# A two-layer encoder on one core: one block product's left operand split a half earlier, first operands fed ahead of the last relu, transposes spread out

## The chip, the core and the metric

The kernel runs on 1 core of one Trainium2 chip, in one launch. The metric is the device time in microseconds (us); lower is better. The engines are called PE (matmul), PEld (its weight load), DVE, ACT, POOL and SP; each works through its own list of instructions in order, and waits on semaphores for the others. A queue name such as SPq or ACTq in a row means that this engine issued a DMA.

## The reference: what is computed

Two rows of 512 tokens (prompt and sample) go through two encoder layers. Each layer has a token mixer, a LayerNorm, a squared-ReLU MLP, and a second LayerNorm:

```python
for l in range(DEPTH):                                # DEPTH = 2, D_MODEL = 1024, D_FF = 4096
    h = x @ w_in[l]
    aq, ak, av, hq, hf_f, hf_b, hi, hg, ga, gb = jnp.split(h, cuts, axis=-1)
    ...
    o_att = window_attention(q, k, v, att_sink[l])
    o_hg = hgrn2_branch(hq, hf_f, hf_b, hi, hg, lower[l], hgrn_norm_g[l])
    mixed = jax.nn.sigmoid(ga) * (o_att @ w_proj_att[l]) + jax.nn.sigmoid(gb) * (o_hg @ w_proj_hgrn[l])
    ...
```

What follows is `layer_norm(ALPHA * x + mixed @ w_out)`, then `layer_norm(ALPHA * x + relu(x @ w_ff1)**2 @ w_ff2)`. All in float32.

## The kernel before, in words

**Products.** A float32 operand is split into a rounded part ("hi", a cast on ACT) and the rest ("lo", a subtraction on DVE or POOL); a product is three matmuls, hi by hi, hi by lo, lo by hi. A projection of 512 tokens on 128 columns is 24 matmuls (`mm3`, L152 to L154). `load_w` loads 512 KB of weights (SP, L143) into one of 3 `raw` tiles and splits them (L131 hi, L132 lo) into one of 3 `w` tiles. `Fm.put(j, rows)` turns 128 finished rows of the activations into columns: 8 transposes on PE (L180), 2 casts on ACT (L185), 2 subtractions on DVE (L186).

**The MLP.** Its first half, `ff1`, makes the 4096 hidden columns in 16 pairs of 256. For each pair `combine` (L904 on) forms sums and differences of four 128x512 tiles, and `spill` writes them to DRAM (`hsp`), since the second product is done by a scheme with seven block products in place of eight. They are the phases M1, M2, M5, M3, M6, M4, M7 of the list `PHASES`, each with 16 steps k, one step for each pair; a step is 12 matmuls (`products`, L971 to L973). `operands` prepares a step's two factors: the left one is loaded from `hsp` into a `raw` tile (SP, L950, 256 KB), the right one is a sum of two blocks of `w_ff2` (POOL, L961); both are then split into a `w` tile, together 128x1024 (L131 on ACT, L132 on DVE). `feed(i)` calls `operands` two steps ahead. M7 is the last phase. Its left factor is the difference of the tiles h2 and h3.

**The end of a layer.** `fold` (L981) adds a finished block to the rows in `acc`. Rows 4 to 7 (of 128 tokens each) are complete when M4 ends, so their LayerNorms (`close`) are called in the steps k = 1, 4, 7, 10 of M7. The last 4 steps of M7 are kept back (`TAIL`, with operands in `X` tiles) and done row by row for rows 0 to 3, with `close` of each row behind the next row's products. A LayerNorm ends with an addition on POOL (L211). `close` then stores: in the first layer to `x_res` (SP, L998) and `put` of the row into the next layer's columns; in the last layer one half of the row by SP and one by ACT (L996). The next layer begins with `prep(0)`: projections on the columns FF, FB and HQ, each for the tokens 512 to 1023 and then for 0 to 511.

**Order.** A scheduler places the instructions on each engine; an engine's order is that of the rows printed in the section on the change, not that of the code.

Of the kernel before, what the change touches and what calls it, by code (L numbers as in the profile page):

```python
# [42 lines left out]
H_M1, H_M2, H_M5, H_M6, H_M7, H_M4, H_M3 = range(7)  # L43
# [44 lines left out]
def tile_encoder_trunk(  # L88
# [17 lines left out]
    hsp = [dram.tile([PAIRS, P, 7, 512], F32, name=f"hsp{l}") for l in range(DEPTH)]  # L106
# [123 lines left out]
    def hgrn(l, x, gate):  # L230
        with tc.tile_pool(name=f"hg{l}", bufs=1) as hp:
# [39 lines left out]

            def prep(p, u):
                for col in (C_FF, C_FB, C_HQ, C_HI, C_HG):
                    if l == 0 and p == 0 and col == C_FF:
                        w = w_first
                    else:
                        w = load_w(
                            [w_in[l][:, col + p * P:col + (p + 1) * P]],
                            *((nc.vector.tensor_copy, nc.vector) if l == 0 and p == 0 and col in (C_FB,) else ()),
                        )  # L280
                    for g in (range(NG), (1, 0))[l > 0 and p == 0]:
                        ps = project(w, x, g)
                        r = u[g]
                        if col in (C_FF, C_FB):
                            d = int(col == C_FB)
                            if not d:
                                r["f"] = hp.tile([P, 2, SEQ], F32, tag="F", name="F", bufs=2)
                                r["k"] = hp.tile([P, 2, SEQ], F32, tag="K", name="K", bufs=4)
                            f = r["f"][:, 1 - d]
                            nc.scalar.activation(out=f, in_=ps, func=AF.Sigmoid)  # L290
                            if l:
                                nc.gpsimd.tensor_scalar(
                                    f, f, oml[:, d, p:p + 1], lb[:, d, p:p + 1], op0=ALU.mult, op1=ALU.add
                                )
                            nc.gpsimd.tensor_scalar(r["k"][:, d], f, -1.0, 1.0, op0=ALU.mult, op1=ALU.add)
                        elif col == C_HQ:
                            sg = t2k()
                            nc.scalar.activation(out=sg, in_=ps, func=AF.Sigmoid)
                            q = t2k()
                            nc.vector.scalar_tensor_tensor(  # L300
                                q, ps, 0.125, sg, op0=ALU.mult, op1=ALU.mult
                            )
                            r["q"] = hp.tile([P, 2, SEQ], F32, tag="Q", name="Q", bufs=4)
                            nc.vector.tensor_tensor(
                                r["q"], q.unsqueeze(1).to_broadcast([P, 2, SEQ]), r["f"], op=ALU.mult
                            )
                            ox = r["ox"] = hp.tile([P, SEQ], F32, tag="ox", name="ox", bufs=4)
                            nc.vector.tensor_tensor(ox, r["k"][:, 0], r["k"][:, 1], op=ALU.add)
                            nc.vector.tensor_tensor(ox, ox, q, op=ALU.mult)
                        elif col == C_HI:  # L310
                            vt = t2k()
                            nc.scalar.copy(vt, ps)
                            ps = sm_ps()
                            for c in range(4):
                                s = slice(c * P, (c + 1) * P)
                                nc.tensor.transpose(ps[:, s], vt[:, s], ident)
                            v = hp.tile([P, 4, P], F32, tag="V", name="V", bufs=2)
                            nc.scalar.copy(v, ps)
                            r["v"] = v
                            pairs(r, vt)  # L320
                        else:
                            sg = t2k()
                            nc.scalar.activation(out=sg, in_=ps, func=AF.Sigmoid)
                            hg = hp.tile([P, SEQ], F32, tag="hg", name="hg", bufs=2)
                            nc.vector.tensor_tensor(hg, ps, sg, op=ALU.mult)
                            r["hg"] = hg
                        yield
# [447 lines left out]

    for l in range(DEPTH):
# [20 lines left out]
        with tc.tile_pool(name=f"ff{l}", bufs=1) as fp:  # L797
# [98 lines left out]
            def ff1(f, out):  # L896
# [186 lines left out]
```

## Time and profile before

| what | us |
|---|---|
| median of 3 runs | 3065.37 (3060.91 to 3068.12) |
| the profiled execution | 3064.09 |
| its span in the trace | 3062.3 |
| PE busy | 2956.7 (97% of the span) |
| DVE, ACT, POOL busy | 1666.7, 1090.9, 865.8 |

The span is that of the trace's instructions; 1.8 us of the profiled execution lie outside it. A busy share is a mean over stages that are bound by different engines. All numbers ahead of the result come from this one execution, whose granted TensorE clock was 0.988 of full speed in the mean.

### The profile page before, as it was taken

The page shows a single profiled execution, that of the slowest core. Times are in us where ns is not written, and L with a number is a line of the kernel's source. Part 1 is how long each engine was busy: PE and PEld are TensorE (multiplying, and loading weights), DVE is VectorE, ACT ScalarE, POOL GpSimd, SP SyncE. Part 2 cuts the span into 40 slices and gives each one's busy share as a digit, 9 for nine tenths or more (in the row PEclk, how much of TensorE's full clock was granted, in tenths as well). Part 3 has the DMA queues.
Part 4 walks back from the last instruction along what each step waited for, and adds up shares of the span by engine and source line. Part 5 has one row for each costly group of instructions (what it writes and reads, how often), then busy time and mean ns, then how long its engine had stood idle before and what let it go on. Part 6 is the DMA issues. An engine that isn't in the chain of part 4 may idle for free.

```text
span 3062.3 us, 42748 instructions
## 1 busy us (share of the span) xinstructions
PE 2956.7 (97%) x16720; PEld 2399.4 (78%) x16720; DVE 1666.7 (54%) x2877; ACT 1090.9 (36%) x1826; POOL 865.8 (28%) x532
## 2 busy tenths in 40 slices
PE   8999999999999999999889999999999999999997
PEld 6777787877888887888667777878878888878885
DVE  5888748126543333445768887481265433344448
ACT  3344447323121112433434444473231211124333
POOL 4222120112222222454542221101231222234544
PEclk9999999999999999999999999999999999999999
DMA  3111232246123346533321112322460243564333
GB/s 127 36 42 36 67 89 69 80 162 218 34 86 134 132 167 241 169 97 97 113 75 36 42 36 69 90 64 100 157 226 9 93 144 125 177 255 144 97 97 107
DMA packets 278890, 331.98 MB, mean 108 GB/s; under 512 B 16545, under 2 KB 185121, under 8 KB 274593
## 3 DMA queue, kind: packets, MB, share of 16 engines
q1 hardware_dynamic: 276816, 325.00, 32.5%
q10 hardware_dynamic: 1872, 4.26, 0.4%
q8 instruction: 131, 2.15, 0.3%
q14 instruction: 71, 0.57, 0.1%
HBM read 230.38 MB, written 92.27 MB: 105 GB/s over the span
## 4 chain that ended last, share of the span: by engine, by line
PE 81%; DVE 10%; DMA 3%; issue 3%; POOL 1%; ACT 1%; SPq 0%; ACTq 0%; POOLq 0%; DVEq 0%
PE mm L152 17%; PE mm L154 16%; PE mm L153 16%; PE sm L971 3%; PE sm L972 3%; PE sm L973 3%; PE mm L972 3%; PE mm L971 3%; PE mm L973 3%; PE mm L864 2%; PE mm L866 2%; PE mm L865 2%; PE sm L695 1%; PE sm L641 1%; PE sm L685 1%
## 5 line engine op out<-in xcount | busy, mean ns | idle before, releaser
L152 PE MATMUL mm<-X,w 128*128 128x512 f32 x2624 | 1033.4, 394 | 4.8 <-ACT w L131 4.1
L153 PE MATMUL mm<-X,w 128*128 128x512 f32 x2624 | 1028.7, 392 | 0.0
L154 PE MATMUL mm<-X,w 128*128 128x512 f32 x2624 | 1026.2, 391 | 1.1 <-POOL w L132 1.1
L132 POOL TENSOR_TENSOR w<-raw,w 128x1024 fp32r<-128x1024 f32 (+1 forms) x179 | 417.9, 2336 | 1370.9 <-ACT w L131 1255.2
L152 PEld LDWEIGHTS mm<-X,w 128*128 128x128 f32 x2624 | 493.6, 188 | 111.8 <-ACT w L131 4.5
L154 PEld LDWEIGHTS mm<-X,w 128*128 128x128 f32 x2624 | 493.8, 188 | 102.3 <-POOL w L132 2.2
L153 PEld LDWEIGHTS mm<-X,w 128*128 128x128 f32 x2624 | 493.8, 188 | 98.6 <-DVE X L793 0.5
L131 ACT CAST w<-raw 128x1024 fp32r<-128x1024 f32 (+1 forms) x330 | 332.1, 1007 | 365.4 <-PE sm L973 106.7
L902 DVE TENSOR_TENSOR X<-t 128x512 f32<-128x512 f32 x128 | 88.6, 692 | 427.8 <-ACT t L901 427.8
L961 POOL TENSOR_TENSOR raw<-X 128x512 f32<-128x512 f32 x160 | 221.8, 1388 | 263.6 <-DVE w L132 259.4
L132 DVE TENSOR_TENSOR w<-raw,w 128x1024 fp32r<-128x1024 f32 x153 | 195.7, 1283 | 168.9 <-ACT w L131 168.7
L901 ACT ACTIVATE t<-mm 128x512 f32<-128x512 f32 x128 | 76.5, 598 | 554.7 <-PE mm L154 546.8
L971 PE MATMUL mm<-w 128*128 128x512 f32 x480 | 190.2, 397 | 11.3 <-ACT w L131 11.3
L972 PE MATMUL mm<-w 128*128 128x512 f32 x480 | 190.3, 396 | 3.7 <-DVE w L132 3.6
L973 PE MATMUL mm<-w 128*128 128x512 f32 x480 | 189.1, 394 | 0.0
L971 PE MATMUL sm<-w 128*128 128x512 f32 x384 | 149.5, 389 | 0.0
L973 PE MATMUL sm<-w 128*128 128x512 f32 x384 | 149.4, 389 | 0.0
L972 PE MATMUL sm<-w 128*128 128x512 f32 x384 | 149.4, 389 | 0.0
L793 DVE TENSOR_TENSOR X<-raw,X 128x512 fp32r<-128x512 f32 x32 | 20.8, 690 | 197.5 <-ACT X L792 197.4
L971 PEld LDWEIGHTS mm<-w 128*128 128x128 f32 x480 | 91.7, 191 | 32.0 <-ACT w L131 12.6
L864 PE MATMUL mm<-X 128*128 128x512 f32 x256 | 103.9, 406 | 11.2 <-DVE t L823 11.2
L959 POOL TENSOR_TENSOR w<-X,w 128x512 fp32r<-128x512 f32 x64 | 85.4, 1334 | 98.8 <-ACT w L955 98.6
(187 smaller groups left out, 3848.9 us busy)
## 6 DMA issues: line engine op xcount, KB each, us to landing
raw<-hsp SPq DMA_DIRECT2D x224, 256.0 KB
raw<-in_w_in_dram SPq DMA_DIRECT2D x84, 512.0 KB
raw<-in_w_ff_dram SPq DMA_DIRECT2D x64, 512.0 KB
hsp<-X SPq DMA_DIRECT2D x32, 1024.0 KB
X<-in_w_ff_dram SPq DMA_DIRECT2D x32, 1024.0 KB
gates<-gt SPq DMA_DIRECT2D x64, 256.0 KB
t<-gates SPq DMA_DIRECT2D x64, 256.0 KB
hsp<-X SPq DMA_DIRECT2D x32, 512.0 KB
```

Of the source, the lines that this page charges most:

```text
L131: (first or nc.scalar.copy)(hi, src)
L132: (eng or nc.gpsimd).tensor_tensor(lo, src, hi.bitcast(F32), op=ALU.subtract)
L152: nc.tensor.matmul(ps, ah, bh, start=(i == 0), stop=False)
L153: nc.tensor.matmul(ps, ah, bl, start=False, stop=False)
L154: nc.tensor.matmul(ps, al, bh, start=False, stop=(i == n - 1))
L864: nc.tensor.matmul(pend[j, n], mh, wh, start=(k == 0), stop=False)
L902: nc.vector.tensor_tensor(out[g], t, t, op=ALU.mult)
L959: nc.gpsimd.tensor_tensor(w[:, 1, 512:], src, w[:, 0, 512:].bitcast(F32), op=ALU.subtract)
L961: nc.gpsimd.tensor_tensor(raw[:, 512:], block(b0, k), block(b1, k), op=op)
L971: nc.tensor.matmul(ps[r], hh, wh, start=first, stop=False, **kw)
L972: nc.tensor.matmul(ps[r], hh, wl, start=False, stop=False, **kw)
L973: nc.tensor.matmul(ps[r], hl, wh, start=False, stop=stop, **kw)
```

## The change

Four things are changed.

1. M7's left factor is split in the first half: `combine` makes its hi (ACT) and lo (DVE) in the tiles where h1 and h2 stood, and `spill` writes 8 slots in two DMAs of 1 MiB, where it wrote 7 slots in three (1 MiB, 512 KB, 256 KB). In M7, `operands` loads both halves (512 KB) straight into the `w` tile, and splits only the right factor, 128x512.
2. `feed(0)` and `feed(1)` are called inside the last `ff1`, ahead of its projections, no longer behind the loop.
3. `put` of rows 4, 5, 6 is called a `close` later, that of row 7 after the first row of the tail, and those of rows 0 to 3 inside the next layer's first `prep`, whose columns now come as FF, FB, HQ for the tokens 512 to 1023 and then FF, FB, HQ for 0 to 511.
4. In the last layer both halves of rows 4 to 7 are stored by SP; rows 0 to 3 as before.

```diff
-H_M1, H_M2, H_M5, H_M6, H_M7, H_M4, H_M3 = range(7)
+H_M1, H_M2, H_M5, H_M6, H_M3, H_M7, H_M7L, H_M4 = range(8)
...
+            def columns(p):
+                cols = (C_FF, C_FB, C_HQ, C_HI, C_HG)
+                order = [(col, g) for col in cols for g in range(NG)]
+                if l and p == 0:
+                    order = [(col, 1) for col in cols[:3]] + [(col, 0) for col in cols[:3]] + order[6:]
+                ws = {}
+                for i, (col, g) in enumerate(order):
+                    if l and p == 0 and i == 3:
+                        for put in puts[2:]:
+                            put()
...
+                    yield col, g, ws[col]
+                    if l and p == 0 and i < 2:
+                        puts[i]()
...
             def ff1(f, out, before=()):
                 w = load_w([w_ff1[l][:, f * P:(f + 1) * P]])
+                for b in before:
+                    b()
...
                 nc.vector.tensor_tensor(h[:, 2], h[:, 2], h[:, 3], op=sub)
+                hi, lo = h[:, 1].bitcast(F32R), h[:, 2].bitcast(F32R)
+                nc.scalar.copy(hi, h[:, 2])
+                nc.vector.tensor_tensor(lo, h[:, 2], h[:, 1], op=sub)
 
             def spill(p, h, s):
                 nc.sync.dma_start(hid[p][:, H_M1:H_M6 + 1], s)
-                nc.sync.dma_start(hid[p][:, H_M7:H_M4 + 1], h[:, 2:4])
-                nc.sync.dma_start(hid[p][:, H_M3], h[:, 0])
+                nc.sync.dma_start(hid[p][:, H_M3:], h)
...
+                w = tile()
+                if slot == H_M7:
+                    nc.sync.dma_start(w[:, :, :512].bitcast(F32), hid[k][:, H_M7:H_M7L + 1])
+                    nc.gpsimd.tensor_tensor(raw[:, 512:], block(b0, k), block(b1, k), op=op)
+                    split(w[:, 0, 512:], w[:, 1, 512:], raw[:, 512:], nc.vector)
+                    return w
...
-                        (nc.sync, nc.scalar)[n].dma_start(yout[g][r * P:(r + 1) * P, h], acc[j][:, h])
+                        (nc.scalar if n and not g else nc.sync).dma_start(
+                            yout[g][r * P:(r + 1) * P, h], acc[j][:, h]
+                        )
                 else:
                     nc.sync.dma_start(x_res[j * P:(j + 1) * P, :], acc[j])
-                    nxt_x.put(j, acc[j])
...
+                    ff1(f, [h[:, 2 * i + g] for g in range(NG)],
+                        [lambda: feed(0), lambda: feed(1)] if f == DFF // P - 1 else ())
...
-            for i in range(ahead):
-                feed(i)
...
                 if ph == END and k % 3 == 1:
                     close(4 + k // 3)
+                    if k > 1 and not last:
+                        nxt_x.put(3 + k // 3, acc[3 + k // 3])
...
                 if r:
                     close(r - 1)
+                elif not last:
+                    nxt_x.put(7, acc[7])
             close(3)
             if not last:
                 xT = nxt_x
+                puts = [lambda j=j, x=nxt_x, rows=acc[j]: x.put(j, rows) for j in range(4)]
```

**ACT at the end of the first layer's `ff1`.** Before, directly behind the last two relus: w_9791, w_9813, w_9831 and so on are the operands of the steps 2, 3, 4 of M1.

```order
L131 CAST w_9791<-raw_9789 128x1024
L131 CAST w_9813<-raw_9811 128x1024
L131 CAST w_9831<-raw_9829 128x1024
L131 CAST w_9849<-raw_9847 128x1024
L131 CAST w_9867<-raw_9865 128x1024
```

With the change, at the same place (L918 is the relu, X_9650 the tile of the last pair):

```order
L131 CAST w_9725<-raw_9724 128x1024
L918 ACTIVATE t512_9755<-mm_9730 128x512
L918 ACTIVATE t512_9783<-mm_9758 128x512
L131 CAST w_9806<-raw_9805 128x1024
L131 CAST w_9828<-raw_9827 128x1024
L929 CAST X_9650<-X_9650 128x512
L131 CAST w_9846<-raw_9845 128x1024
```

The last pair's new hi copy (L929) stands behind the casts of steps 2 and 3; the casts of steps 0 and 1 stand ahead of the last relus, as they did before.

**SP in M7 of the first layer.** Before: the loads of steps 7 to 11 into `raw` tiles (L950; those of the steps ahead of 7 stand ahead of all stores), and the stores of rows 4 to 6 (L998).

```order
L950 DMA raw_11783<-hsp0_70 128x512
L998 DMA x_res_67<-acc_7261 128x1024
L950 DMA raw_11801<-hsp0_70 128x512
L950 DMA raw_11819<-hsp0_70 128x512
L998 DMA x_res_67<-acc_7344 128x1024
L950 DMA raw_11867<-hsp0_70 128x512
L950 DMA raw_11885<-hsp0_70 128x512
L998 DMA x_res_67<-acc_7427 128x1024
```

With the change: the loads of steps 3 to 10 into `w` tiles (L954; those of the tail stand further ahead, in M4), and the stores of rows 4 to 7 (L1007).

```order
L954 DMA w_11664<-hsp0_70 128x2x512
L954 DMA w_11698<-hsp0_70 128x2x512
L1007 DMA x_res_67<-acc_7261 128x1024
L954 DMA w_11716<-hsp0_70 128x2x512
L954 DMA w_11734<-hsp0_70 128x2x512
L1007 DMA x_res_67<-acc_7344 128x1024
L954 DMA w_11786<-hsp0_70 128x2x512
L1007 DMA x_res_67<-acc_7427 128x1024
L954 DMA w_11804<-hsp0_70 128x2x512
L954 DMA w_11822<-hsp0_70 128x2x512
L1007 DMA x_res_67<-acc_7510 128x1024
L954 DMA w_11870<-hsp0_70 128x2x512
```

The loads of the steps 5 and 6 now stand behind row 4's store, that of step 7 behind row 5's, those of 8 and 9 behind row 6's, those of 10 and 11 behind row 7's.

**ACT at the end of the last layer.** Before, with two of the stores of rows 4 to 7 (L996; out_1 is the second output) between the casts:

```order
L996 DMA out_1_dram<-acc_19358 128x512
L202 ACTIVATE rs_23814<-mv_23812 128x1
L131 CAST w_23757<-raw_23755 128x1024
L131 CAST X_23793<-raw_23791 128x1024
L131 CAST w_23775<-raw_23773 128x1024
L207 ACTIVATE acc_19441<-acc_19441,nb_23817,rs_23814 128x512
L131 CAST X_23828<-raw_23826 128x1024
L996 DMA out_1_dram<-acc_19441 128x512
L131 CAST X_23846<-raw_23844 128x1024
```

With the change, the same stretch:

```order
L131 CAST X_23824<-raw_23823 128x512
L131 CAST w_23788<-raw_23787 128x512
L131 CAST X_23859<-raw_23858 128x512
L131 CAST X_23877<-raw_23876 128x512
L131 CAST w_23806<-raw_23805 128x512
L131 CAST X_23883<-raw_23882 128x512
L202 ACTIVATE rs_23919<-mv_23917 128x1
```

No store of rows 4 to 7 is left among ACT's casts; they stand on SP, between M7's loads in the way of the rows above, each row as two stores of 256 KB.

## Rows read from the trace of the kernel before

**Rows 1.** The page's costliest groups: busy, mean ns, idle before and its releaser.
```profile
L971 PE MATMUL mm<-w 128*128 128x512 f32 x480 | 190.2, 397 | 11.3 <-ACT w L131 11.3
```

**Rows 2.** First M7 to sixth projection: PE, PEld, DVE, ACT, POOL busy, clock, DMA.
```profile
1470.00:1582.00 112.00, 95.01 (x411) 75.78 (x410) 78.89 (x113) 40.28 (x59) 55.21 (x41) 0.92 0.33 106
```

**Rows 3.** PE's waits from 1469 to 1582: total, times, longest.
```profile
PE sm L180 <- POOL acc L211: 14.5, 7, 4.2
```

**Rows 4.** The same stretch in windows of 5 us.
```profile
1485.00:1490.00 5.00, 5.00 (x19) 4.08 (x18) 1.96 (x4) 1.74 (x3) 0.84 (x1) 0.69 0.45 157
...
1515.00:1520.00 5.00, 3.02 (x9) 2.57 (x10) 4.61 (x5) 1.59 (x3) 1.93 (x1) 0.54 0.33 116
...
1550.00:1555.00 5.00, 4.32 (x14) 3.26 (x13) 2.79 (x5) 2.02 (x4) 1.96 (x2) 0.50 0.44 179
```

**Rows 5.** ACT in order of time, first layer's end: start, duration, instruction, idle before.
```profile
1468.96 1.05 ACT L131 CAST w<-raw 128x1024 fp32r<-128x1024 f32 x1 [1.67 <-PE mm L973]
1471.68 1.05 ACT L131 CAST w<-raw 128x1024 fp32r<-128x1024 f32 x1 [1.67 <-PE mm L973]
...
1507.34 1.05 ACT L131 CAST X<-raw 128x1024 fp32r<-128x1024 f32 x1 [2.51 <-DMA raw<-hsp]
...
1523.74 1.05 ACT L131 CAST w<-raw 128x1024 fp32r<-128x1024 f32 x1 [4.08 <-DMA raw<-in_w_in_dram]
...
1554.26 1.28 ACT L290 ACT_TABLE_LOAD   x1 [0.83 <-DMA x_res<-acc]
...
1581.57 0.60 ACT L298 ACTIVATE t2k<-mm 128x512 f32<-128x512 f32 x1 [4.84 <-PE mm L154]
```

**Rows 6.** SP's DMA issues in order of time, first layer's end.
```profile
1484.64 0.32 SPq L998 DMA_DIRECT2D x_res<-acc  x1
...
1503.42 0.32 SPq L998 DMA_DIRECT2D x_res<-acc  x1
1504.50 7.76 SPq L950 DMA_DIRECT2D raw<-hsp  x4
...
1519.90 10.12 SPq L143 DMA_DIRECT2D raw<-in_w_in_dram  x4
```

**Rows 7.** DVE in order of time, from the first fold of the first layer's M4.
```profile
1469.59 0.69 DVE L981 TENSOR_TENSOR acc<-acc,mm 128x512 f32<-128x512 f32 x1 [1.04 <-PE mm L973]
...
1477.41 0.14 DVE L203 RECIPROCAL rs<-rs 128x1 f32<-128x1 f32 x1
...
1479.44 1.22 DVE L132 TENSOR_TENSOR w<-raw,w 128x1024 fp32r<-128x1024 f32 x1
1480.58 0.68 DVE L209 TENSOR_TENSOR acc<-acc,t 128x512 f32<-128x512 f32 x1
```

**Rows 8.** ACT's waits from 2991 to the end: total, times, longest.
```profile
ACT rs L202 <- POOL acc L211: 7.5, 2, 4.7
...
ACT X L131 <- POOL acc L211: 5.8, 1, 5.8
...
ACT w L131 <- POOL acc L211: 3.5, 1, 3.5
```

**Rows 9.** DVE in order of time, last layer: folds of M4 and of the tail.
```profile
2991.72 0.69 DVE L981 TENSOR_TENSOR acc<-acc,mm 128x512 f32<-128x512 f32 x1 [1.04 <-PE mm L973]
...
3039.27 0.69 DVE L981 TENSOR_TENSOR acc<-acc,mm 128x512 f32<-128x512 f32 x1 [1.31 <-PE mm L973]
```

**Rows 10.** POOL in order of time, last layer's M7.
```profile
3004.52 2.27 POOL L211 TENSOR_TENSOR acc<-acc,t 128x512 f32<-128x512 f32 x1
```

**Rows 11.** The chain of waits from 1200 to 1226: start, duration, what.
```profile
1205.09 0.61 DVE X L910
...
1205.72 5.87 DMA hsp<-X
...
1212.40 8.27 DMA raw<-hsp
```

**Rows 12.** Busy time in a window of 3 us inside PE's wait there.
```profile
1218.00:1221.00 3.00, 0.00 (x0) 0.00 (x0) 0.00 (x0) 0.23 (x1) 0.00 (x0) 0.58 1.05 406
```

More of the change, by code (lines that the diff above doesn't have):

```diff
@@ L105, in tile_encoder_trunk @@
     o_sp = [dram.tile([8, P, NG * SEQ], F32, name=f"o_sp{l}") for l in range(DEPTH)]
-    hsp = [dram.tile([PAIRS, P, 7, 512], F32, name=f"hsp{l}") for l in range(DEPTH)]
+    hsp = [dram.tile([PAIRS, P, 8, 512], F32, name=f"hsp{l}") for l in range(DEPTH)]
     gates = [dram.tile([2, KT, P, NG * SEQ], F32, name=f"gates{l}") for l in range(DEPTH)]
@@ L270, in pairs @@
                     nc.gpsimd.tensor_tensor(ox, ox, w, op=ALU.add)
-            def prep(p, u):
-                for col in (C_FF, C_FB, C_HQ, C_HI, C_HG):
-                    if l == 0 and p == 0 and col == C_FF:
-                        w = w_first
-                    else:
[L277 to L327, printed above, removed]
@@ new lines, in columns @@
+            def columns(p):
[8 more added lines that the diff above has]
+                            put()
+                    if col not in ws:
+                        if l == 0 and p == 0 and col == C_FF:
+                            ws[col] = w_first
+                        else:
+                            ws[col] = load_w(
+                                [w_in[l][:, col + p * P:col + (p + 1) * P]],
+                                *((nc.vector.tensor_copy, nc.vector) if l == 0 and p == 0 and col in (C_FB,) else ()),
+                            )
+                    yield col, g, ws[col]
+                    if l and p == 0 and i < 2:
+                        puts[i]()
@@ L774, in x_rows @@
         return x_res[j * P:(j + 1) * P, :]
+    puts = []
     for l in range(DEPTH):
@@ L894, in page, with ff1 @@
                 return tile(dt).rearrange("p (k t) -> p k t", t=512)
-            def ff1(f, out):
+            def ff1(f, out, before=()):
                 w = load_w([w_ff1[l][:, f * P:(f + 1) * P]])
+                for b in before:
+                    b()
                 for g in range(NG):
@@ L926, in block @@
                 return blocks[b[0], b[1], k // 4][:, k % 4]
-            early = [(b, c) for c in range(4) for b in ((0, 0), (1, 1))]
-            done = []
-            for p in range(PAIRS):
-                if p >= PAIRS - 4:
-                    for b, c in early[:1]:
-                        load_block(*b, c, a_tile)
-                    early = early[1:]
-                h, s = page(a_tile), page(a_tile)
-                for i in range(2):
-                    ff1(2 * p + i, [h[:, 2 * i + g] for g in range(NG)])
-                combine(h, s)
-                done.append((p, h, s))
-                if len(done) > 1:
-                    spill(*done.pop(0))
-            spill(*done.pop(0))
-            for b, c in early:
-                load_block(*b, c, a_tile)
             late = [((i, 1 - i), c) for i in range(2) for c in range(4)]
@@ L1010, in feed @@
                     ready.append(operands(ph, k, (lambda: a_tile(F32R).rearrange("p (a n) -> p a n", a=2)) if tail else w_tile))
+            early = [(b, c) for c in range(4) for b in ((0, 0), (1, 1))]
+            done = []
+            for p in range(PAIRS):
+                if p >= PAIRS - 4:
+                    for b, c in early[:1]:
+                        load_block(*b, c, a_tile)
+                    early = early[1:]
+                h, s = page(a_tile), page(a_tile)
+                for i in range(2):
+                    f = 2 * p + i
+                    ff1(f, [h[:, 2 * i + g] for g in range(NG)],
+                        [lambda: feed(0), lambda: feed(1)] if f == DFF // P - 1 else ())
+                combine(h, s)
+                done.append((p, h, s))
+                if len(done) > 1:
+                    spill(*done.pop(0))
+            spill(*done.pop(0))
+            for b, c in early:
+                load_block(*b, c, a_tile)
             ahead = 2
-            for i in range(ahead):
-                feed(i)
             later, banks = [], {}
```

48 lines of the change are left out of this document (47 added, 1 removed).

## The prediction

> **What bounds the kernel now.** I read the page first: PE is busy 97% of the span, so only stretches in which PE stands still or runs slowly can give time, or take it. One group there shows a wait at the start of each second product: the matmuls of L971 waited 11.3 us for ACT in the whole run [rows 1]. PE's waits and the windows show the others, at the ends of the layers.
>
> *End of the first layer.* From the first fold at t0 = 1469.6 [rows 7] to the sixth projection's end at 1581.6 [rows 5] are 112 us. The work in it, on PE alone: a step of 12 matmuls takes 2.72 us (two casts that each wait for the step before them are that far apart [rows 5]), so 0.227 for a matmul. M7 is 16 steps, 43.5; six projections of 24 matmuls are 32.7; together 76.2. The 64 transposes are 16 groups of four, four matmul times or some 0.45 each with their weight loads: 7.2, an estimate. That makes 83.4; 28.6 us are lost. PE's waits name 14.5 of them: transposes waiting for the LayerNorm's last addition [rows 3]. In the windows, about 17 us of PE are idle (112 less 95.0 [rows 2]), and behind the longer gaps the granted clock is 0.69, 0.54 and 0.50 for stretches of 5 us [rows 4], where the level of 1.2 GHz is mixed in; this explains the rest, with the transposes' own pace.
>
> *End of the last layer.* From M4's first fold, 2991.7, to the tail's first fold, 3039.3, are 47.6 us [rows 9], where 13 steps need 35.4. 12.2 are lost. ACT stood 3.5, 7.5 and 5.8 us for POOL's additions [rows 8], at instructions behind its own output stores: a store waits for its row, and the casts of M7 wait behind the store.
>
> *Start of the second product.* The chain of waits goes through the last spill (5.87 us from its issue to landing) and a first load of 8.27 us [rows 11]; meanwhile the DMA engines are full, 406 GB/s at a share of 1.05 [rows 12]. So this wait is one for bytes.
>
> **The change part by part.**
>
> *The split moved into `ff1`.* Each of 32 pairs gets a 128x512 copy on ACT (0.6, as an activation of that shape [rows 5]) and a subtraction on DVE (0.68 [rows 7]). A pair lasts 96 matmuls, 21.8 us, so this lies beside PE. If the cover were gone it would cost 32 x 1.3 = 41 us at most; I take nothing, but for the last pair. There the hi copy stands on ACT behind the casts of steps 2 and 3, the latter of which waits for PE to finish step 0, and lo follows on DVE; I work out the last spill's issue as some 2.9 us later than 1205.7 [rows 11]. It also carries 1 MiB in place of 512 KB. The queue is still full at that time (5.87 us are some 2.4 MB at 406 GB/s [rows 11, 12]), so the delay is the bytes: 512 KB at 406 GB/s, 1.3, with a little for the order, **+1.5 a layer, +3**. Lower bound +1.3; upper bound, if the queue runs dry, 2.9 + 1.3 = 4.2, which makes +8.4 for both.
>
> *The early feeds.* The order of ACT has the casts of steps 0 and 1 ahead of the last relus before and after. Nothing, or the few tenths that the relu would wait for a cast of 1.05 [rows 5].
>
> *The transposes.* In M7 each `put` came just behind its `close`, so PE met it before POOL was done. Afterwards there is a `close` between them, and rows 0 to 3 stand behind whole projections of 5.4 us. The 14.5 us go, and with them most of the slow clock. What is late next? Two things.
>
> First, M7's loads. They now go straight into a `w` tile, which PE frees only at the end of a step, and SP has the stores of rows 4 to 7 ahead of them. Each load becomes ready this long after it is issued: landing, cast 0.6, subtraction 0.65. For the landing of 512 KB I have two rows: a 256 KB load behind a 512 KB store took 2.84 (1504.50 to 1507.34), a 512 KB load 3.84 (1519.90 to 1523.74) [rows 5, 6]; I take 3.3. With 0.4 for the issue that is **4.95** from a store's release to the operand. Freed tiles alone leave no wait: 5.44 us are two steps, 4.55 are needed.
>
> When is row 4 done? Before, its L209 ended at 1481.3, t0 + 11.7 [rows 7], and its store went at t0 + 15.0 [rows 6]. Four subtractions of 1.22 [rows 7] stand in these 11.7; afterwards two of them, of half the size, stand ahead of L209, but step 3's must wait for its load (tile free at t0 + 2.7, ready at 7.3). From there the rest of the LayerNorm takes 2.6 (1477.4 to 1481.3 without a subtraction [rows 7]), and POOL's addition up to 2.27 [rows 10], of which I take 1.8: the store goes at about t0 + 11.7. Step 5's operand is then ready at 16.6, where PE comes to it at 14.5 (five steps and row 4's transposes): a wait of 2.1. Row 5's LayerNorm has its L209 behind that subtraction on DVE: L209 0.7 and L211 end at 18.9, step 7 is ready at 23.9, PE is there at 22.0: 1.9. By the same steps (on DVE each LayerNorm waits in line with these subtractions) row 6 ends at 24.2, step 8 is ready at 29.2 against 27.5: 1.7; row 7 at 32.4, step 10 at 37.4 against 34.6: 2.8. M7 is paced by the LayerNorms, by **8.5 us**. Bounds: 2 if the loads land in 2 us less and LayerNorms run ahead; 16 if each wait doubles.
>
> Second, the start of the next layer. The activations F, F and q now stand on ACT behind the casts of rows 2 and 3, with a table load of 1.28 and three times 0.6 [rows 5] ahead of the last cast that the fourth projection needs: some **3 us** for PE, bounds 1 and 5.
>
> So 83.4 + 8.5 + 3 = 94.9 in place of 112.0: **-17** (bounds -25 and -9).
>
> *Stores and narrower casts in the last layer.* ACT no longer stands at stores, and M7 goes by the same loads behind stores of SP, here in halves, without transposes to cover: the first wait is 0.9 longer, the third as much, but 256 KB less stand ahead of a load (0.6 at 406 GB/s [rows 12]). I take 8: 35.4 + 8 = 43.4 for 47.6, **-4.2** (bounds -10, with 2 us of waits, and +2). Behind the tail's first fold nothing changes: 23 us to the end (3039.3 [rows 9] to the span's 3062.3) are DVE's LayerNorms and the last stores.
>
> The Trainium skill says, on the page "DMA: Bandwidth & Descriptors", section "Issuing engines are not separate DMA queues", that DMAs of all engines end on the same 16 DMA engines, and that issuing from several saves only the sequencer's issue time, usually small. By it the stores' move from ACT to SP would be worth next to nothing, and the sum some -14. The row speaks against it: 16.8 us of ACT at three such waits [rows 8] are not issue time but in-order waiting behind a store, which the rule leaves out.
>
> Sum: +3 - 17 - 4.2 = -18.2 on the profiled execution of 3064.1, which lies 1.3 below the median: 3045.9, say **3046**.
>
> **The rivals.**
>
> *A. The loads are not late (22%).* Then the waits in both M7 are 2 each: -23.6 - 10.2 + 3, about 3033. For it: before, loads fed two steps ahead were mostly in time. Against: the order on SP has each behind a store that waits for POOL.
>
> *B. The boundary costs its upper bound (13%).* The chain of waits grows by 4.2 a layer in place of 1.5: 3051. For it: the hi copy stands behind a cast that waits for PE. Against: the share of 1.05 [rows 12], at which a late issue is hidden by queued bytes.
>
> *C. The gain of the spread transposes is eaten (10%)*, each wait in M7 double, with the clock falling behind them as it did behind the gaps before [rows 4]: -9 + 2 + 3, about 3060 at the worst, 3056 in the middle.
>
> *D. The direct load rules M7, and it is slower (4%).* One `w` tile of three is used for 2.72, then loaded and split again (L + 1.25), so a step lasts (3.97 + L) / 3, above 2.72 from L = 4.2. My forecast's 8.5 us over some eight steps are a pace of 3.8; to lose another 18.2 in both layers it must be 4.9, that is L = 10.8 for every load. The longest load here took 8.27, with the DMA engines full [rows 11]; in M7 their share is near 0.33 [rows 2]. At L = 12 a step is 5.3 us, another 1.5 x 16 = 24, and the time 3070.
>
> *E. The early feeds move something after all.* A cover for the 11.3 us [rows 1] isn't in the order; no chance of its own.
>
> **How the numbers follow.** A change of this kernel can be told from none by about 0.2%, 6 us. My forecast, 50%, is 3046 (its own range 3040 to 3052). The range must leave out 20%: it goes down to A's 3033 and up past B to most of C, **3033 to 3058**. Faster by over 6 us is the forecast, A, B and half of C: 0.89. Within 0.2%: the rest of C and a little of D: 0.07. Slower: D's worse end, 0.04.
>
> **What would show it.** PE's waits at L180 for L211 should be gone, and in M7 waits for DVE's or ACT's operands at the steps 5, 7, 8 and 10 should stand in their place, each below 3 us, with SP's stores just ahead. ACT should show no L211 wait before the tail's end. At the start of the second product PE should wait some 7 us in place of 5.7, behind a later spill. The prediction is wrong if M7's loads land in under 2.5 us or above 5, if the last spill is issued after the queue ran dry, or if the fourth projection of layer two waits for something that I haven't seen.

## The result and the profile after

| | before | changed |
|---|---|---|
| median, us | 3066.11 (4 runs, 3060.91 to 3068.12) | 3050.67 (4 runs, 3046.43 to 3051.77) |
| profiled span, us | 3062.3 | 3049.3 |

The ratio is 0.995, with a 95% interval of 0.9932 to 0.9967: 15 us faster. 3046 had been forecast, with a range of 3033 to 3058.

One table carries most of what follows. It cuts the execution into stages by PE's rows: each number is the time from the start of one named matmul to the start of the next.

```
us, profiled execution                                        before   after
start to M1's first matmul, first layer                      1202.24 1201.89
M1's first matmul to its ninth step (at least 21.8)            29.72   34.97
to M7's first matmul                                          239.47  239.45
M7's first to its last matmul                                  67.35   51.65
to the last matmul of the next layer's sixth projection        42.36   38.23
to that of its twentieth                                      108.09  110.92
to M1's first matmul, last layer                             1035.34 1036.05
M1's first matmul to its ninth step                            29.50   32.43
to M7's first matmul                                          239.49  239.45
M7's first to its last matmul                                  54.45   49.89
to the end                                                     14.30   14.41
```

The end of the first layer gives 15.7 + 4.1, and 2.8 are lost again in the projections behind it; the last layer's M7 gives 4.6; the two starts of the second product take 5.3 and 2.9. With the small rest that is -13.0, the difference of the spans.

The same lines as before, now of the changed kernel. PE's waits in the first layer's M7 (1476 to 1528), which answer to [rows 3]:

```profile
PE mm L978 <- DMA w<-hsp: 2.6, 2, 2.1
```

No transpose waits for POOL's L211 any more. In the windows there, in place of the three slow stretches of [rows 4], one is left, around the one wait of 2 us (columns: PE, PEld, DVE, ACT, POOL busy, granted clock, DMA share, GB/s):

```profile
1500.00:1505.00 5.00, 2.95 (x14) 2.36 (x13) 3.08 (x5) 1.32 (x2) 4.05 (x3) 0.85 0.65 219
1505.00:1510.00 5.00, 5.00 (x19) 3.99 (x19) 3.00 (x5) 2.73 (x5) 3.54 (x3) 0.81 0.87 295
```

SP's issues in order of time, which answer to [rows 6]: M7's loads (L954) leave right behind the stores (L1007), as the order had it.

```profile
1486.11 0.33 SPq L1007 DMA_DIRECT2D x_res<-acc  x1
1486.60 1.55 SPq L954 DMA_DIRECT2D w<-hsp  x2
1491.93 0.33 SPq L1007 DMA_DIRECT2D x_res<-acc  x1
1492.38 0.37 SPq L954 DMA_DIRECT2D w<-hsp  x1
1497.86 0.33 SPq L1007 DMA_DIRECT2D x_res<-acc  x1
1498.31 1.18 SPq L954 DMA_DIRECT2D w<-hsp  x2
1504.47 0.33 SPq L1007 DMA_DIRECT2D x_res<-acc  x1
1504.90 3.01 SPq L954 DMA_DIRECT2D w<-hsp  x2
```

The chain of waits at the start of the second product, which answers to [rows 11]:

```profile
1205.41 1.09 DVE w L132
1206.50 1.10 issue
1207.60 1.80 DVE X L930
1209.39 0.02 issue
1209.41 4.93 DMA hsp<-X
...
1214.82 10.59 DMA raw<-hsp
```

The last spill leaves 3.7 us later than before (1209.41 for 1205.72), behind a subtraction for step 3 and the new lo (L930), and the load behind it takes 10.59 in place of 8.27. In the last layer the same load takes 7.88, where it took 8.22:

```profile
2726.22 7.88 DMA raw<-hsp
```

Around the first layer's last spill the DMA engines move less than in the kernel before. Changed, and then before:

```profile
1209.00:1212.00 3.00, 3.00 (x15) 2.49 (x14) 2.62 (x2) 0.00 (x0) 1.84 (x2) 1.00 0.74 298
1212.00:1215.00 3.00, 3.00 (x15) 2.49 (x14) 0.00 (x0) 0.00 (x0) 0.99 (x1) 1.00 0.96 294
```

```profile
1209.00:1212.00 3.00, 3.00 (x15) 2.45 (x15) 1.23 (x1) 0.00 (x0) 3.00 (x3) 1.00 1.00 375
1212.00:1215.00 3.00, 3.00 (x15) 2.49 (x14) 0.00 (x0) 0.00 (x0) 0.63 (x1) 1.00 1.05 399
```

At 298 and 294 GB/s in place of 375 and 399, 6 us move 0.55 MB less, 1.3 us at 406 GB/s. Only the first of the two windows, with a share of 0.74, shows idle DMA engines; with the last pair whole (an experiment below) they move 425 and 305 at shares of 1.02. PE's wait there is 11.0 us, where it was 5.9; the rest of its row, 8.3, is that of the last layer, where it was 5.4:

```profile
PE mm L978 <- ACT w L131: 19.3, 2, 11.0
```

### The profile page after: what moved, and what is told of

The parts are those of the page before. It is cut to its first block, busy times and chain, and to the rows that moved or that the text cites. A ratio compares the mean times of both kernels' runs of the same rounds, so it can differ in the third digit from the quotient of the medians.

```text
span 3049.3 us, 42766 instructions
## 1 busy us (share of the span) xinstructions
PE 2950.1 (97%) x16720; PEld 2398.4 (79%) x16720; DVE 1668.9 (55%) x2909; ACT 1092.6 (36%) x1858; POOL 862.1 (28%) x532
## 4 chain that ended last, share of the span: by engine, by line
PE 82%; DVE 11%; DMA 3%; issue 2%; ACT 1%; POOL 1%; SPq 0%; POOLq 0%; ACTq 0%; DVEq 0%
PE mm L152 17%; PE mm L154 16%; PE mm L153 16%; PE mm L978 3%; PE mm L979 3%; PE sm L978 3%; PE sm L979 3%; PE sm L980 3%; PE mm L980 3%; PE mm L879 2%; PE mm L881 2%; PE mm L880 2%; PE sm L709 1%; PE sm L655 1%; PE sm L699 1%
## 5 line engine op out<-in xcount | busy, mean ns | idle before, releaser
L131 ACT CAST w<-raw 128x1024 fp32r<-128x1024 f32 (+1 forms) x330 | 321.2, 975 | 374.9 <-PE sm L980 106.6
L132 DVE TENSOR_TENSOR w<-raw,w 128x1024 fp32r<-128x1024 f32 (+1 forms) x153 | 184.4, 1210 | 174.3 <-ACT w L131 174.2
L968 POOL TENSOR_TENSOR raw<-X 128x512 f32<-128x512 f32 x128 | 173.7, 1359 | 227.9 <-DVE w L132 226.2
L918 ACT ACTIVATE t<-mm 128x512 f32<-128x512 f32 x128 | 76.5, 598 | 422.7 <-PE mm L154 422.7
```

The costliest lines, as they stand in the source:

```text
L131: (first or nc.scalar.copy)(hi, src)
L132: (eng or nc.gpsimd).tensor_tensor(lo, src, hi.bitcast(F32), op=ALU.subtract)
L968: nc.gpsimd.tensor_tensor(raw[:, 512:], block(b0, k), block(b1, k), op=op)
```

## The experiments

In the profiled executions the first 1200 us, in which they hardly differ, took between 1198.9 and 1205.3 us, so parts are compared by the stages of the table above, and whole times by medians. Ratios are to the kernel before, run beside it on the same chip.

### The parts alone, or undone

**The transposes alone** (the kernel before with the third part of the change).

> The kernel before with the third part of the change alone (the transposes later, the first columns of the next layer in two passes). My reasons: the wait for POOL's addition at the transposes (14.5 us) goes, the start of the second product and the last layer stay as they were. In the first layer M7 takes 67.4 us from its first step to its last in the kernel before and 51.7 with the whole change; if the transposes alone were the cost, it is 52 to 54 here and the time about 3049, as short as with the whole change, since the 4 to 8 us that the split costs at the start of the second product are not paid and the 4.6 us of the last layer are missing. Rival (DVE, which is full there with subtractions of 1.22 us, paces M7, and the narrower split is what gives): M7 stays near 60 and the time near 3057.

3052.91, ratio 0.9951 (0.9939 to 0.9964): as much as the whole change. M7 of the first layer 52.1, the starts of the second product 30.9 and 30.5, M7 of the last layer 55.2. The rival falls: once the transposes are moved, DVE with its wide subtractions does not pace the first layer's M7. PE's waits in that M7 are small and of DVE alone:

```profile
PE mm L972 <- DVE X L132: 2.3, 2, 1.3
PE mm L972 <- DVE w L132: 1.5, 1, 1.5
```

**The split alone** (the kernel before with the first part).

> The kernel before with the first part alone: M7's left factor split in the first half. My reasons: both starts of the second product cost some 3.5 us more, M7 of the first layer still waits at the transposes (13 to 15 us), the last layer gains 1 or 2 from narrower casts: 3066 to 3071, no faster than before. Rival (DVE's work is the pace): M7 of the first layer falls by 6 us or more, and the time to 3060.

3061.08, ratio 0.998 (0.9971 to 0.9989): somewhat faster, and here the rival was right about the first layer. M7 there is 59.4 in place of 67.4: the waits at the transposes, in M7 and the projections behind it, shrink from 16 us (14.5 of them in [rows 3]) to 7, though the transposes stand where they stood.

```profile
PE sm L180 <- DVE mv L200: 3.6, 1, 3.6
PE sm L180 <- POOL acc L211: 3.2, 2, 2.0
...
PE sm L180 <- DVE acc L210: 0.5, 1, 0.5
```

M7 of the last layer is 50.2, with ACT still issuing every other store. The starts are 35.2 and 34.7, 10.7 us dearer in all. So in this profile the split alone gains about 12 us in the two M7 and pays 11 for them (it is the slowest of the run's eleven executions, 3065.24, and its stages do not show the 5 us of the medians); where the transposes are moved too, its gain in the first layer is already taken.

**The stores back on ACT** (the changed kernel without the fourth part).

```diff
-                        (nc.scalar if n and not g else nc.sync).dma_start(
+                        (nc.sync, nc.scalar)[n].dma_start(
```

> The changed kernel with the fourth part undone: in the last layer the second halves of the rows 4 to 7 are stored by ACT again. If ACT's waiting behind the stores was what cost there, M7 of the last layer goes from 49.9 back to 52 or more, and the time up by 2 to 5 us. By the rule that an issuing engine saves only its issue time, nothing changes, 3050.7 within 0.1%.

3051.02, ratio 0.9948 (0.9935 to 0.996): no difference; M7 of the last layer 50.25. ACT again stands at the stores, and it costs nothing:

```profile
ACT rs L202 <- POOL acc L211: 3.6, 1, 3.6
ACT w L131 <- POOL acc L211: 3.2, 1, 3.2
...
PE mm L978 <- DMA w<-hsp: 3.6, 2, 2.8
PE mm L979 <- DVE w L132: 0.6, 2, 0.4
```

The first two rows are ACT's waits behind its stores in that M7, 6.8 us where the kernel before had 16.8 [rows 8]; the last two are all of PE's.

**The feeds back behind the loop** (the changed kernel without the second part).

> The changed kernel with the second part undone: the first two operands are fed behind the loop. I expect no difference, 3050.7 within 0.1%, and the start of the second product (first matmul to the ninth step) 32 to 35 us as with the whole change. Rival (the earlier feeds are what brings the loads of steps 2 and on behind more bytes): the start goes to 30 or 31 us in both layers, and the time falls by some 3 us.

3052.06, ratio 0.9948 (0.9935 to 0.996), the starts 35.1 and 32.2: nothing, as expected.

### What the start of the second product costs

**The last pair whole.** Its left factor goes the old way, in three DMAs and with a split in the tail.

```diff
+                if not part:
+                    return
                 hi, lo = h[:, 1].bitcast(F32R), h[:, 2].bitcast(F32R)
...
+                if p == PAIRS - 1:
+                    nc.sync.dma_start(hid[p][:, H_M7L:], h[:, 2:4])
+                    nc.sync.dma_start(hid[p][:, H_M3], h[:, 0])
+                else:
+                    nc.sync.dma_start(hid[p][:, H_M3:], h)
...
-                combine(h, s)
+                combine(h, s, p < PAIRS - 1)
```

> The last pair's left factor for M7 goes the old way: no hi and lo in the first half, its spill is 1 MiB, 512 KB and 256 KB again, and its step of M7 (one of the tail) loads and splits the whole. Theory (the last pair's spill is late behind ACT's cast and carries 512 KB more): PE's wait at the start of the second product goes back from 11.0 and 8.4 us to about 5.9 and 5.4, the time falls by about 8 us, to 3042 or 3043. Rival one (the wider row pitch of hsp, 16 KiB, or the more bytes of the other 15 pairs slow the DMA engines there): the waits stay near 11 and 8, the time within 2 us of the changed kernel's. Rival two (the early feeds reorder the DMAs): the same, no change.

The starts fall to 32.0 and 31.1, PE's waits to 7.4 and 6.1; the spill again leaves 3.28 us behind the last relu's start, as before. The load behind it leaves 11.2 us behind M1's first matmul in both layers, where it left 12.9 and 13.1 in the changed kernel and 10.2 and 9.8 before. So the late and larger last spill is 1.8 and 1.9 of the 2.8 and 3.3 us by which that load was late. The time does not follow: 3053.04, ratio 0.9966 (0.9953 to 0.9978). That one step of M7 now needs the cast and subtraction of its left factor behind a late load, and M7 takes 53.4 and 53.5, 1.7 and 3.6 more: PE's waits for loads in the whole run are 10.7 us in nine places, where they were 5.8 in five.

**The last pair's hi on DVE.**

```diff
-                combine(h, s)
+                combine(h, s, *([nc.vector.tensor_copy] if p == PAIRS - 1 else []))
```

> Only the last pair's hi copy goes from ACT to DVE, so that hi and lo stand on one engine and no cast of a later step is ahead of them on ACT; the spill is still two DMAs of 1 MiB. If lateness is the cost, the last spill is issued near 1206.5 instead of 1209.4 and the waits fall to about 7 us each: 3046 or so. If the bytes are the cost, the waits stay at some 10 and 8 us and the time within 2 us of the changed kernel's.

3053.51, ratio 0.9965 (0.9951 to 0.9979); starts 35.0 and 34.0. This tells nothing of lateness against bytes, for the spill did not leave earlier: lo (L930) ran at 1212.45, 6.9 us behind the start of the last relu, where it ran 5.5 behind it in the changed kernel.

**A pitch of 18 KiB.**

```diff
-    hsp = [dram.tile([PAIRS, P, 8, 512], F32, name=f"hsp{l}") for l in range(DEPTH)]
+    hsp = [dram.tile([PAIRS, P, 9, 512], F32, name=f"hsp{l}") for l in range(DEPTH)]
...
-                nc.sync.dma_start(hid[p][:, H_M3:], h)
+                nc.sync.dma_start(hid[p][:, H_M3:H_M4 + 1], h)
```

> The scratch tensor hsp has nine slots in place of eight, one of them never written or read, so that a row's pitch is 18 KiB and not 16 KiB; nothing else changes. My theory says no difference, 3050.7 within 0.2%, and a first wait of 11.0 us. If the power-of-two pitch slows the spill and the loads at the start of the second product, the first wait shrinks toward 7 us and the time falls by 4 to 8 us.

3051.69, ratio 0.9963 (0.995 to 0.9975): within its spread of the changed kernel. The starts are 32.6 and 32.2; the first is 2.4 below that of the changed kernel's one profile, but stores_by_pool below, whose pitch is 16 KiB, has 32.8 there. So this stage itself varies by some 2 us (where that comes from is in the section on the prediction), and the pitch is not shown to matter.

**The late blocks held back.** Eight blocks of w_ff2 (8 MiB) that M1 does not need are loaded during M1; three had been issued ahead of the last spills.

```diff
+                if behind is not None:
+                    pool_copy(t[:, 0, :1], behind)
...
-                    load_block(*b, c, c_tile)
+                    load_block(*b, c, c_tile, raws[-1][:, 512:513])
```

> The changed kernel, in which the eight blocks of w_ff2 that M3 and later phases need (8 MiB, the loads called late in the code) can't be loaded before a step of M1: POOL writes one element of each block's tile first, behind its addition for that step. In the changed kernel three of them (3 MiB) were issued from 1193.7 to 1197, just ahead of the last spills and of step 5's load. Theory (the wait at the start of the second product is bytes in the DMA queue, so that whatever stands ahead of step 5's load costs 1 us for 0.4 MB): the start (first matmul to ninth step) falls from 35.0 and 32.4 us to some 27 in both layers, and the time by 10 to 13 us, to 3038 to 3041. Rival (the wait is the chain of relu, sums, hi, lo, spill, and the block load that waits for it): the start falls by 1 or 2 us at most, since that chain stays.

The start falls by 2.4 us in the first layer (32.6, which pitch_18k has too) and not at all in the last (32.5), and the rest of the phases up to M7 grows by 1.3 and 2.1 (240.7 and 241.5, where every kernel that holds no blocks back has 239.4 to 239.5). 3053.75, ratio 0.9966 (0.9952 to 0.9979). The theory, 10 to 13 us for 3 MiB less ahead of one load, was too simple: 2.4 came at one start, and the phases behind both starts lost 1.3 and 2.1.

**The same, and step 5's load ahead of the last block loads.**

```diff
-            for b, c in early:
+            for b, c in early[:-2]:
...
+                if ph == 0 and k in (2, 4):
+                    b, c = early.pop(0)
+                    load_block(*b, c, a_tile)
```

> As late_blocks_held, and two of the blocks that M1 needs at its ninth and thirteenth step are loaded inside M1, behind the operands' loads, so that step 5's load no longer waits on SP for the block load that waits for the last spill to land. If bytes are all, this gives 1 or 2 us more than late_blocks_held or nothing; if the wait on SP behind the spill is what counts, this one gives most of the gain and late_blocks_held little: the start at 22 to 24 us, the least possible for eight steps being 21.8.

Starts of 31.3 and 31.1, and 240.9 and 241.9 up to M7; 3053.38, ratio 0.9961 (0.9948 to 0.9973). PE's wait for step 5 is 5.9 us in the first layer, but the loads in the chain of waits then still took over 7 us, this one and two behind it (7.16 and 7.24):

```profile
1210.17 7.88 DMA raw<-hsp
```

From 1215 to 1240 the DMA engines have a share of 1.05 throughout. That M1's first part is bound by what they have to move until the blocks are in fits this, and is not shown beyond it.

**Transposes alone, late blocks held.**

> The kernel before with the third part of the change alone (as puts_only), and the late blocks held back as in late_blocks_held. It tells what the split costs at the start of the second product once the queue is not full: the start should be within 1 us of late_blocks_held in both layers, the last layer's M7 55 us, so that the time is about 4 us above late_blocks_held.

Starts of 31.2 and 30.1, in both layers below late_blocks_held by 1.3 and 2.4, M7 of the last layer 55.0; 3054.42, ratio 0.997 (0.9958 to 0.9981). The split costs at the start even so; against 4.1 and 1.9 with all in the queue, and with a stage that varies by 2 us, it is not shown to cost less.

### Two versions that might have beaten both

**M7's stores by POOL.** L1003 and L1007 of the rows 4 to 7 on POOL's queue.

```diff
-                        (nc.scalar if n and not g else nc.sync).dma_start(
+                        (nc.gpsimd if g else (nc.sync, nc.scalar)[n]).dma_start(
...
-                    nc.sync.dma_start(x_res[j * P:(j + 1) * P, :], acc[j])
+                    (nc.gpsimd if g else nc.sync).dma_start(x_res[j * P:(j + 1) * P, :], acc[j])
```

> The stores of rows 4 to 7 are issued by POOL, behind its own last addition of the row, and no longer by SP, in both layers: M7's loads no longer stand behind a store. Theory (what PE still waits for in M7 is the load issued behind the store): the waits of 2.6 and 3.1 us for loads in the two M7 go to under 1, with the slow clock behind them: 5 to 8 us faster than the changed kernel, 3043 to 3046. Rival (M7 is paced by the LayerNorms on DVE, or issuing DMAs costs POOL as much as it gives): no change, or slower by some us through later additions on POOL.

Both theories had a half. The waits for loads are gone, and waits for the splits take their place; of the last layer's M7:

```profile
PE mm L979 <- DVE w L132: 3.8, 4, 1.4
PE mm L978 <- ACT w L131: 2.5, 2, 1.7
```

M7 of the first layer is 50.6 (1.1 less), that of the last 53.4 (3.5 more). There POOL holds a store for half a microsecond and some more around it, between the additions that the splits wait for:

```profile
2992.16 0.60 POOL L1003 DMA_DIRECT2D out_dram<-acc  x1 [0.85 <-DVE mv L200]
2993.22 1.66 POOL L211 TENSOR_TENSOR acc<-acc,t 128x512 f32<-128x512 f32 x1 [0.46 <-DVE acc L209]
2995.18 0.56 POOL L1003 DMA_DIRECT2D out_dram<-acc  x1 [0.30 <-POOL acc L211]
```

3059.97, ratio 0.9981 (0.9972 to 0.999), 9 us slower than the changed kernel. The profiled execution, at 3054.87, is the fastest of eleven, so its stages show only 3.7 of the 9 us; where the others lie is open.

**The split in the last layer alone**, where the transposes do not take its gain.

```diff
-                combine(h, s)
+                combine(h, s, last)
...
-                if slot == H_M7:
+                if slot == H_M7 and not last:
+                    slot = H_M7L
+                if slot == H_M7:
```

> The changed kernel with the early split in the last layer alone; the first layer's M7 splits its left factor as the kernel before does, behind the moved transposes. From the stages of the runs so far: the first layer's start of the second product 30 to 31 us (35.0 with the split, 30.9 with the transposes alone), its M7 52 (52.1 with the transposes alone, 51.7 with both), the last layer as in the changed kernel (start 32.4, M7 49.9). If the parts add, it is 3 to 4 us faster than the changed kernel, 3047. If the split gives back elsewhere what it costs at the start, within 1 us of it.

The four stages came as they were expected (31.4, 52.1, 32.4, 49.9), but the stage behind the first layer's M7 is 40.0 and not 38.2, as it is with the transposes alone (40.05): half of what the start had given is missing there. That this is the split's is not sure, since pitch_18k, stores_by_pool and late_blocks_held_raw_first, with the split in both layers, have 40.2 to 41.8 there. 3052.28, ratio 0.9951 (0.9937 to 0.9964): no better than the changed kernel. No version ran that beats it.

## Why the prediction was right, and where it was not

**The sum.** -18.2 was forecast on the profiled execution's own time, and -13.0 came in the spans, -15.4 in the medians. The sign and the place were right: the transposes' wait is the gain. The terms were off in both directions.

**Start of the second product: mis-sized, and rival B in its place.** +3 was taken, +8.2 came (5.3 and 2.9), next to the upper bound of 8.4 which rival B had for it; 3051 was B's time, and 3050.7 was measured. The failed step is "The queue is still full at that time", from which "the delay is the bytes" was taken. The trace has the delay at the load behind the last spill, which leaves 2.8 and 3.3 us later behind M1's first matmul than before: the queued bytes did not hide the late spill. The spill itself leaves 4.0 us later by that measure, not 2.9, and not for hi, which B had in mind: lo stood behind DVE's subtraction for step 3 and took 1.80 itself, beside an addition of POOL's, where such a subtraction takes 0.68 elsewhere (the last section). With the last pair whole, 1.0 and 1.4 of the lateness were still there. The other 15 pairs spill 256 KB more each; that this is the rest was argued, not shown.

What remains of the first layer's 5.3 is that load's landing. The trace marks a landing in sixteen steps. In the first and the last layer, the first mark comes 7.1 and 7.3 us behind the load's issue, the fifteenth 8.4 and 7.8, and the sixteenth 10.6 and 7.9: one part of the load is late. In the profiles with as late a spill and no blocks held back, a start is 32.2 to 32.6 us where the marks lie within 0.6 us (the first layer of pitch_18k, the last layer of most), and 34.7 to 35.2 where they lie 1.9 or more apart (32.8 and 34.5 at 1.4 and 1.5). Why one part is late in some executions is open. Where none is, a start is 1.3 to 3.1 us above those of the kernel before and of the transposes alone (29.5 to 30.9).

**End of the first layer: about the right gain, by other terms.** -17 was taken; M7 and the six projections behind it came out 19.8 shorter, and 2.8 were lost again right behind them. That the net is -17.0 is luck. Row 4's store was forecast for t0 + 11.7. M4's last step began at 1473.6 (M7's first matmul at 1476.3, less one step) and its first fold could run 0.9 later (1469.6 against a step that began at 1468.7), so t0 is 1474.5, though the fold ran at 1475.1, behind a subtraction; the store left at 1486.1, t0 + 11.6. The way from a store to the operand behind it was forecast as 4.95, and PE went on 5.4 us behind row 4's store (1486.11 to 1491.53) and 5.0 behind row 6's (1497.86 to 1502.90). This is right in size and wrong in kind. The loaded half needs no "cast 0.6, subtraction 0.65"; PE waits for the landing itself, as its row says (w<-hsp), and the landing is longer than 3.3:

```profile
1498.31 4.46 DMA w<-hsp
```

One of the two rows that 3.3 was taken from is a load issued 1.1 us behind its store (1504.50 against 1503.42 [rows 6]), not right behind it.

Yet M7's waits are 2.6 us, not 8.5: 0.6 at step 5, 2.1 at step 8, none at 7 and 10. Two steps failed. First, t0 is M4's first fold, 1.8 us ahead of M7's first matmul; the 83.4 us of pure work should have been 85.2, and PE comes to each step that much later than I had it. Second, "step 3's must wait for its load": the subtraction left in M7 is that of the right factor, which does not come with the load. So DVE is not held up by late loads, and the stores of rows 5, 6 and 7 left at t0 + 17.4, 23.4 and 30.0, where their rows were to end at 18.9, 24.2 and 32.4. The +3 for the next layer's fourth projection, a part of the -17, came as 1.4, at the hi and lo of the last transposes:

```profile
PE mm L153 <- DVE X L186: 1.1, 1, 1.1
PE mm L152 <- ACT X L185: 0.3, 1, 0.3
```

The slow clock behind M7's longest wait had no term: the step that had waited took 4.4 us in place of 2.7, at clocks of 0.85 and 0.81. 85.2 and 2.6, 1.4 and 1.7 are 90.9, of the 92.2 (112.0 less 19.8) that this end now takes. The waits in both M7, 2.6 and 3.7, are nearer to rival A's 2 each than to the forecast, but not for its reason: loads behind stores do come late.

**The stage behind.** That something is lost there was not in the prediction. In all profiles of kernels with moved transposes, the fourteen projections behind the sixth take 109.4 to 112.3 us, 1.3 to 4.2 more than in the one profile of before, and the 1035 us behind them 0.4 to 2.9 more. But the split alone, whose transposes stand where they stood, has 109.5 and 2.0 more too, so the moved transposes are not shown to be the cause. In the changed kernel's trace PE waits 5.2 us in that stage for DVE's t2k, for 4.0 before, and the granted clock is 0.86 for 10 us behind the longest of these waits. Why DVE is later there is not settled.

**Last layer: the right sum, half the cause.** -4.2 was taken and -4.6 came in M7. It had been put down to the stores' move together with the narrower casts. With the stores back on ACT it stays (50.25), with the split alone it is there (50.2), with the transposes alone it is not (55.2): it is the split's. PE's waits in that M7, before and then changed:

```profile
PE mm L972 <- DVE w L132: 3.6, 3, 1.5
PE mm L971 <- ACT X L131: 1.9, 1, 1.9
```

```profile
PE mm L978 <- DMA w<-hsp: 3.1, 3, 2.4
PE mm L979 <- DVE w L132: 0.6, 1, 0.6
```

From M4's first fold to the tail's first it is 43.4 us (2983.84 to 3027.20), the very number of the forecast, and that is luck: of the 8 us above 13 steps the waits are 3.7, and the rest lies at the stage's two ends and in the slow clock behind the longest wait (0.72 from 3010 to 3015). The rule of the Trainium skill, "DMA: Bandwidth & Descriptors", section "Issuing engines are not separate DMA queues", by which the stores' move is worth next to nothing, gave the right outcome against my reading of [rows 8]. The waits of ACT were real, but an engine that stands behind stores costs only what is late behind it; with the left factor no longer cast by ACT, nothing was, and the 6.8 us that ACT waits with the stores back made PE wait for nothing. Whether the stores' move would have given something without the split, where ACT waited 16.8 us, was not tried.

**The feeds** gave nothing, as the order had shown. **Rival D**, the slower one, did not come near: loads in M7 make PE wait 2.4 us at most.

**What the parts are worth.** Moved transposes: the whole gain; the new order of the next layer's columns came with them, and the two were not tried apart. The split, beside them (the changed kernel against the transposes alone): it gives 5.3 us in the last layer's M7 and 0.5 in the first layer's, and takes 4.1 and 1.9 at the two starts, a balance smaller than their times can tell. The changed kernel is also 1.8 shorter behind the first layer's M7, but of the nine profiles with the split in both layers and the transposes moved five have 38.2 to 38.3 in that stage and four 39.1 to 41.8, so this is not shown to be the split's. Feeds and stores: nothing.

## What to carry to other kernels

Two edits that take away the same wait do not add: the split alone cut the first layer's M7 by 8 us, the transposes alone by 15, both together by 16, and the split's price at the starts was paid all the same. Work moved beside a busy engine cost nothing that shows inside its loop (1202.24 us before and 1201.89 after to the end of the first layer's `ff1`), but it cost at the loop's last item, where the next phase stands behind it. And before a wait of an engine is counted as a cost, look for who is late because of it: ACT's 6.8 us behind its stores (with the stores back) cost nothing, once its casts were not the last thing that a step waited for.

## What the hardware showed beside this

DVE's operations on two operands take more than twice as long where POOL has started an operation of the same kind just before. In the last layer's M7 of the changed kernel, DVE's and then POOL's rows:

```profile
2989.36 0.73 DVE L208 SCALAR_TENSOR_TENSOR acc<-acc,mv,t 128x512 f32<-128x512 f32 x1
...
2993.65 1.71 DVE L208 SCALAR_TENSOR_TENSOR acc<-acc,mv,t 128x512 f32<-128x512 f32 x1
...
2995.41 1.66 DVE L210 SCALAR_TENSOR_TENSOR acc<-acc,rs,t 128x512 f32<-128x512 f32 x1
...
2999.49 1.71 DVE L132 TENSOR_TENSOR w<-raw,w 128x512 fp32r<-128x512 f32 x1
```

```profile
2989.45 1.79 POOL L955 TENSOR_TENSOR raw<-X 128x512 f32<-128x512 f32 x1 [1.16 <-DVE rs L203]
2993.13 1.68 POOL L211 TENSOR_TENSOR acc<-acc,t 128x512 f32<-128x512 f32 x1 [1.89 <-DVE acc L209]
2994.77 1.74 POOL L955 TENSOR_TENSOR raw<-X 128x512 f32<-128x512 f32 x1
...
2999.36 1.29 POOL L211 TENSOR_TENSOR acc<-acc,t 128x512 f32<-128x512 f32 x1
```

L208 takes 0.73 us where it starts 0.09 ahead of POOL's L955, and 1.71 where it starts behind L211 (1.68); the subtraction that takes 0.68 elsewhere takes 1.71 behind L211. The Trainium skill, on the page "SBUF — State Buffer", section "SBUF: two separate sides", says that DVE, with two inputs in SBUF, and POOL take turns at a shared pair of ports, each holding it for a whole instruction. The rows fit: each of the three longer ones ends 0.55 us behind POOL's instruction (2995.36 and 2994.81, 2997.07 and 2996.51, 3001.20 and 3000.65), as if it had begun its work there. And L955, which takes 1.29 at its shortest here, takes 1.79 where DVE's L208 had started first. So a LayerNorm's length in M7 depends on when POOL makes the right factors, and durations taken from a stretch without POOL are too short for it.
